# Moving a forget gate and its broadcast reads to an earlier place in a two-block hybrid attention kernel

## The chip, the cores and the metric

The kernel runs on one core of a Trainium2 chip. The metric is the device time of one execution in microseconds. Before the change the median of three runs is 1819.09 us, with 1818.62 and 1819.64 us as the lowest and highest.

## The reference

The program computes two blocks on a sequence of 512 tokens of 1024 features, in float32. The first block has two layers (`hybrid_layer`, l = 0 and 1). Each layer normalizes `x`, multiplies it by `w_in`, and feeds three kinds of attention: differential, stick-breaking and forgetting. Their outputs, gated by SiLU, are multiplied by `w_out`, normalized and added to `x`. The second block (a linear recurrence, a dilated attention and a feed-forward) is not touched here.

What matters here is the forgetting attention, and above all the cumulated log of its forget gate, which is added to the logits:

```python
log_f = jax.nn.log_sigmoid((ff + f_bias).astype(jnp.float32)).transpose(0, 2, 1)
cum_log_f = jnp.cumsum(log_f, axis=-1)
...
logits = jnp.einsum('bhqd,bhkd->bhqk', q[:, :, q0:q1], k[:, :, :q1]).astype(jnp.float32) * scale
logits = logits + cum_log_f[:, :, q0:q1, None] - cum_log_f[:, :, None, :q1]
```

`ff` holds 8 columns of the product with `w_in`, one for each of the 8 forgetting heads. The term of the query row falls out of the softmax, so the kernel adds only the key's term: one row of 512 numbers for each head.

## The kernel before, in words

**Products.** Every float32 operand is split into a high part (rounded, by ScalarE, line 219) and a low part (the rest, by VectorE and GpSimd, line 233), and each product is made of three TensorE products: high by high, high by low, low by high (`mm3`). Weights come in units of 128 x 1024 numbers: SP loads a unit into one of two `raw` buffers (line 203), and its parts go to one of four buffers of `wh` and `wl`. The normalized input stands in `hTH` and `hTL`, features on partitions.

**The order of the work.** The 12 head pairs of a layer (0 to 3 differential, 4 to 7 stick-breaking, 8 to 11 forgetting) each need three projections (`projections(n)`: q, k and the gate, one unit and 24 products of 512 columns each, called a chunk), and each two pairs need a value product (`values`, `value_steps`). The projections are generators that a filler (`Filler`) holds in one list in the order in which they were added: projections of pairs 1 to 11, with the value products of pairs 4, 6, 8 and 10 before the pair that needs them, and last the first half of the product with `w_out`. `spread` runs the attention steps of pair n, four of them, and between the stages of a step lets the filler go on up to a goal in chunks. The goals are such that the projections of pair 8 run while the attention steps of pair 7 do; the last of these projections is done shortly before the first attention step of pair 8.

Every TensorE product is made by `matmul` (line 126) or `transpose` (line 143), and both tie it behind the product written before, so TensorE's order is that of the Python program:

```python
def matmul(*args, **kw):
    tc.keep_in_program_order(nc.tensor.matmul(*args, **kw))
```

The other engines' instructions are ordered by a scheduler in the framework, which takes what is ready, the earlier written first; each engine then runs its list in order.

**The forget gate.** The value product of pair 8 has 264 columns instead of 256: the last 8 are the forget gates. `value_steps` adds the bias to them (line 569) into `ff`, 128 x 32. The generator `forget_gate` then makes softplus of it on VectorE with one Exp on ScalarE (`softplus_neg`, `log1p_exp_neg`, lines 480 to 503: one instruction each at lines 480, 484, 485, 487, 489, 491, seven pairs at lines 493 and 494, lines 495, 502 and 503), transposes the result by four TensorE transposes (line 639, recorded at line 143), copies and scans it on VectorE (lines 641 and 643) and writes it to the DRAM tile `cum` (line 645). In the kernel before, this generator is added after the three projections of pair 8.

**The broadcast reads.** In stage `a` of step 0 of each forgetting pair, `pair_step` has SP read one row of `cum` for each of the two heads, broadcast to 128 partitions (line 740), into tiles of the tag `bc`, which has four buffers; the forget gate uses two of these for its own input and output. Each score tile then gets the mask (line 747), and line 758 adds the broadcast and takes the row maximum. For a stick-breaking pair the score tile goes through lines 750 to 755. Stage `b_` transposes the weights and copies them (line 511), stage `c` makes the product with the values.

Of the kernel before, what the change touches and what calls it, by code (L numbers as in the profile page):

```python
# [16 lines left out]
P = 128  # L17
S = 512
# [70 lines left out]
def hybrid_kernel(ctx, tc, A, out):  # L89
    nc = tc.nc  # L90
# [11 lines left out]
    def nm(tag):  # L102
        count[0] += 1
        return f"{tag}_{count[0]}"
# [3 lines left out]
    def work(tag, dt=F32, shape=(P, S)):  # L108
        return ap.tile(list(shape), dt, tag=tag, bufs=BUFS[tag], name=nm(tag))
# [161 lines left out]
    def feature_steps(key, done, src=None, ps=None, span=(0, S)):  # L271

        wh, wl = key if isinstance(key[0], Slab) else unit(*key)
        if ps is None:
            ps = bank()
        nk = KD if src is None else len(src)
        lo, hi = span
        for k in range(nk):
            if src is None:
                mH, mL = hTH[:, k, lo:hi], hTL[:, k, lo:hi]  # L280
            else:
                mH, mL = src[k][0][:, lo:hi], src[k][1][:, lo:hi]
            c = slice(P * k, P * (k + 1))
            mm3(ps[:, lo:hi], wh[:, c], wl[:, c], mH, mL, k == 0, k == nk - 1)
            yield 1.27 * (hi - lo)
        if done is not None:
            done(ps)
# [284 lines left out]
    def hybrid_layer(l, vs0):  # L572
# [20 lines left out]
        st = {}  # L593

        def projections(n):

            kind, idx = n // 4, n % 4
            base = 4 * W_GRP * kind + P * idx
            s = st[n] = {}
            gens = []  # L600

            def put(name, scale):
                def done(ps):
                    pair = y_tile(F32R)
                    t = ps
                    if kind == 0:
                        t = work("e")
                        ACT.activation(t, ps, AF.Copy, scale=scale)
                        rope(t, P, shuffle8, cosT, sinT)
                    rest = None if name == "q" else klow[n % 2]  # L610
                    for b in range(2):
                        own = slice(64 * b, 64 * b + 64)
                        other = slice(64 - 64 * b, 128 - 64 * b)
                        cols = slice(S * b, S * b + S)
                        h = pair[own, cols]
                        lo = pair[other, cols] if name == "q" else rest[own, cols]
                        if kind == 0:
                            ACT.copy(h, t[own])
                            V.tensor_tensor(lo, t[own], h.bitcast(F32), op=ALU.subtract)  # L619
                        else:  # L620
                            ACT.activation(h, ps[own], AF.Copy, scale=scale)
                            V.scalar_tensor_tensor(lo, ps[own], scale, h.bitcast(F32), ALU.mult, ALU.subtract)
                        if name == "k":
                            evict(pair[other, cols], h.bitcast(F32))
                    s[name] = (pair, rest)

                return done

            def put_gate(ps):
                sg = work("sg")  # L630
                ACT.activation(sg, ps, AF.Tanh, scale=0.5)
                V.scalar_tensor_tensor(sg, sg, 1.0, ps, ALU.add, ALU.mult)
                s["sg"] = sg

            def forget_gate(ff):
                sp_f = softplus_neg(ff, 32)
                ffT = bank()
                for t in range(4):
                    transpose(ffT[0:8, P * t : P * (t + 1)], sp_f[:, 8 * t : 8 * t + 8])
                cum_in = work("bc")  # L640
                V.tensor_copy(cum_in[0:8], ffT[0:8])
                cum = work("bc")
                V.tensor_tensor_scan(cum[0:8], cum_in[0:8], cum_in[0:8], 0.0, ALU.add, ALU.bypass)
                st["cum"] = dp.tile([8, S], F32, tag="cum", bufs=2, name=nm("cum"))
                nc.sync.dma_start(st["cum"], cum[0:8])
                yield 0.0

            gens.append((CHUNK, feature_steps(("w_in", l, ((base, P),), 0, 8), put("q", 0.125))))
            gens.append((CHUNK, feature_steps(("w_in", l, ((base + W_GRP, P),), 0, 8), put("k", 1.0))))
            if kind == 0:  # L650
                s["vs"] = vs0[2 * (idx // 2) : 2 * (idx // 2) + 2]
            else:
                s["vs"] = st["vs", n - idx % 2]
            gens.append((CHUNK, feature_steps(("w_in", l, ((base + 3 * W_GRP, P),), 0, 8), put_gate)))
            if n == 8:
                gens.append((0.0, forget_gate(st["ff"])))
            return gens

        def values(n):
# [70 lines left out]
        def pair_step(n, i):  # L730
            s = st[n]
            loc = {}

            def a():
                if n >= 8 and i == 0:
                    s["bc"] = []
                    for b in range(2):
                        hd = 2 * (n - 8) + b
                        bc = work("bc")
                        nc.sync.dma_start(bc, st["cum"][hd : hd + 1, :].to_broadcast((P, S)))  # L740
                        s["bc"].append(bc)
                pss, w = scores(s, i)
                loc["w"] = []
                for b in range(2):
                    ps = pss[b]
                    mask = causal if n >= 8 else strict
                    V.tensor_tensor(ps[:, w - P : w], ps[:, w - P : w], mask, op=ALU.add)
                    e = work("e")
                    if n < 8:
                        ACT.activation(e[:, :w], ps[:, :w], AF.Sigmoid)  # L750
                        keep = work("e")
                        V.tensor_scalar(keep[:, :w], e[:, :w], -1.0, 1.0, ALU.mult, ALU.add)  # L752
                        rev = keep[:, :w][:, ::-1]
                        V.tensor_tensor_scan(rev, rev, rev, 1.0, ALU.mult, ALU.bypass)  # L754
                        V.tensor_tensor(e[:, : w - 1], e[:, : w - 1], keep[:, 1:w], op=ALU.mult)  # L755
                    else:
                        mx = stat()
                        V.tensor_tensor_reduce(e[:, :w], ps[:, :w], s["bc"][b][:, :w], 1.0, -3e38, ALU.add, ALU.max, mx)  # L758
                        V.tensor_scalar(mx, mx, -1.0, None, ALU.mult)  # L759
                        den = stat()  # L760
                        ACT.activation(e[:, :w], e[:, :w], AF.Exp, bias=mx, accum_out=den)  # L761
                        r = stat()
                        V.reciprocal(r, den)
                        V.tensor_scalar(e[:, :w], e[:, :w], r, None, ALU.mult)
                    loc["w"].append(e)

            def b_():
                if i == 0:
                    s["wT"] = {}
                for b in range(2):  # L770
                    if i == 1:
                        t = s["wT"][0, b]
                        transpose_evict(loc["w"][b], 2, dst=t[:, P : 3 * P])
                        s["wT"][1, b] = t[:, P : 3 * P]
                    else:
                        s["wT"][i, b] = transpose_evict(loc["w"][b], i + 1)

            def c():
                if i % 2 == 0:
                    return  # L780
                if i == 1:
                    s["o"] = bank()
                o = s["o"]
                for q in (i - 1, i):
                    for j in range(q + 1):
                        for b in range(2):
                            matmul(
                                o[64 * b : 64 * b + 64, P * q : P * (q + 1)],
                                s["vs"][n % 2][:, P * j + 64 * b : P * j + 64 * b + 64],
                                s["wT"][q, b][:, P * j : P * (j + 1)],  # L790
                                start=j == 0,
                                stop=j == q,
                            )
                if i == 3:
                    sg = s["sg"]
                    V.scalar_tensor_tensor(sg, o, 0.5, sg, ALU.mult, ALU.mult)
                    chunks[n] = split(sg, "yT")

            return [a, b_, c]
# [122 lines left out]
    vs0, gens = values0(0)  # L922
# [77 lines left out]
    for l in range(2):  # L1000
# [21 lines left out]
        if l == 0:  # L1022
            vs0, gens = values0(1)
# [7 lines left out]
    hd = {}  # L1031
# [448 lines left out]
```

## Time and profile before

| What | Value |
|---|---|
| median of 3 runs | 1819.09 us (1818.62 to 1819.64) |
| the profiled execution | 1817.58 us |
| its span | 1815.8 us |
| TensorE products (PE) | 1770.9 us busy |
| VectorE (DVE) | 1131.9 us busy |
| ScalarE (ACT) | 765.1 us busy |
| GpSimd (POOL) | 647.9 us busy |
| mean granted clock of TensorE | 0.992 |

Times in the profile are microseconds from the start of the span. L126 is line 126 of the kernel. In a row of the timeline the first number is the start, the second the time taken, then engine, line, operation, output and input tiles by their names (`ps` a PSUM bank, `sm` a small tile, `wT` a transposed weight tile), shapes and a count; a bracket at the end is the idle time of the engine just before, and what ended it. The granted clock is a share of TensorE's full 2.4 GHz. TensorE's busy time counts matmuls that overlap in the pipeline, so the distance between two starts says more than the duration of one.

### The profile page before, as it was taken

What the parts mean: (1) busy time and instruction counts of PE and PEld (TensorE: products, weight loads), DVE (VectorE), ACT (ScalarE), POOL (GpSimd) and SP (SyncE); (2) the same over time, 40 slices, a digit from 0 to 9 for tenths busy, and PEclk for the clock granted to TensorE, in tenths of its full rate; (3) what the DMA queues carried; (4) which work ended last, traced back from release to release, by engine and by line L of the source; (5) the groups of instructions that cost most, each with busy time, mean ns of one, the idle gap of its engine ahead of it and who ended that gap; (6) DMA issues with size and microseconds to landing.
All of it is one profiled execution on the core that took longest, in us unless ns stands there. A gap on an engine that the chain in (4) does not pass through costs nothing.

```text
span 1815.8 us, 26033 instructions
## 1 busy us (share of the span) xinstructions
PE 1770.9 (98%) x9774; PEld 1519.8 (84%) x9774; DVE 1131.9 (62%) x2450; ACT 765.1 (42%) x1461; POOL 647.9 (36%) x534
## 2 busy tenths in 40 slices
PE   9989998999998999899999999999999999999998
PEld 8778887888977888788899888878788888888898
DVE  5888898775588899776682677886433632222122
ACT  4545444443355544444433333677522432232221
POOL 3333212222333222122253555344554344444331
PEclk9999999999999999999999999999999999999999
DMA  5212222322321322222223223223323223332321
GB/s 202 92 47 82 65 76 82 93 70 72 123 76 53 93 60 70 94 93 83 71 88 116 82 77 99 82 71 105 110 83 117 97 93 93 103 95 94 103 94 70
DMA packets 51695, 162.12 MB, mean 89 GB/s; under 512 B 8481, under 2 KB 10049, under 8 KB 51570
## 3 DMA queue, kind: packets, MB, share of 16 engines
q1 hardware_dynamic: 51570, 160.46, 27.9%
q8 instruction: 77, 1.26, 0.3%
q14 instruction: 48, 0.39, 0.1%
HBM read 158.28 MB, written 2.16 MB: 88 GB/s over the span
## 4 chain that ended last, share of the span: by engine, by line
PE 76%; DVE 12%; ACT 3%; issue 3%; DMA 2%; POOL 2%; SPq 0%; POOLq 0%; DVEq 0%; ACTq 0%
PE ps L126 73%; PE ps L143 3%; DVE wl L233 2%; DVE e L754 1%; POOL e L522 1%; DMA raw<-in_wu_dram 1%; ACT wh L219 1%; DVE e L755 1%; DMA bc<-cum 1%; DVE e L520 1%; POOL st L361 1%; DVE yT L523 0%; DVE e L752 0%; DVE st L690 0%; DVE klow L619 0%
## 5 line engine op out<-in xcount | busy, mean ns | idle before, releaser
L233 POOL TENSOR_TENSOR wl<-raw,wh 128x368 fp32r<-128x368 f32 (+5 forms) x262 | 362.6, 1386 | 654.0 <-ACT wh L219 614.0
L126 PE MATMUL ps<-hTH,wh 128*128 128x512 f32 (+1 forms) x1336 | 533.2, 399 | 1.4 <-DVE sm L1128 1.4
L126 PE MATMUL ps<-hTH,wl 128*128 128x512 f32 (+1 forms) x1336 | 522.9, 391 | 0.0
L126 PE MATMUL ps<-hTL,wh 128*128 128x512 f32 (+1 forms) x1336 | 522.6, 391 | 0.0
L219 ACT CAST wh<-raw 128x1024 fp32r<-128x1024 f32 (+2 forms) x263 | 269.0, 1026 | 400.9 <-PE ps L126 227.7
L233 DVE TENSOR_TENSOR wl<-raw,wh 128x656 fp32r<-128x656 f32 (+6 forms) x261 | 257.9, 989 | 286.2 <-ACT wh L219 284.6
L126 PEld LDWEIGHTS ps<-hTH,wl 128*128 128x128 f32 x1336 | 253.0, 189 | 54.7
L126 PEld LDWEIGHTS ps<-hTH,wh 128*128 128x128 f32 x1336 | 253.9, 190 | 49.2 <-issue 1.6
L126 PEld LDWEIGHTS ps<-hTL,wh 128*128 128x128 f32 x1336 | 253.8, 190 | 47.1
L126 PE MATMUL ps<-wh,yT 128*128 128x512 f32 (+1 forms) x544 | 161.4, 369 | 0.0
L126 PEld LDWEIGHTS ps<-wh,yT 128*128 128x128 f32 x544 | 98.5, 189 | 15.9 <-issue 0.3
L126 PE MATMUL ps<-wh,hTH 128*128 128x256 f32 (+2 forms) x496 | 106.2, 302 | 3.1 <-DVE sm L716 1.6
L361 POOL TENSOR_TENSOR st<-st,half_neg 128x1 f32<-128x1 f32 x64 | 37.6, 587 | 196.0 <-DVE st L359 114.2
L126 PE MATMUL ps<-wl,hTH 128*128 128x256 f32 (+2 forms) x496 | 106.7, 300 | 0.4 <-POOL wl L233 0.4
L126 PE MATMUL ps<-wh,hTL 128*128 128x256 f32 (+2 forms) x496 | 105.3, 300 | 0.0
L126 PE MATMUL ps<-wl,yT 128*128 128x512 f32 (+1 forms) x272 | 99.2, 365 | 0.0
L126 PEld LDWEIGHTS ps<-wh,hTH 128*128 128x128 f32 x496 | 84.7, 208 | 4.9 <-DVE sm L716 2.0
L126 PEld LDWEIGHTS ps<-wl,hTH 128*128 128x128 f32 x496 | 84.5, 207 | 0.9 <-POOL wl L233 0.6
L126 PEld LDWEIGHTS ps<-wh,hTL 128*128 128x128 f32 x496 | 83.8, 207 | 0.1
L126 PE MATMUL ps<-y,y 128*128 128x128 f32 (+2 forms) x240 | 70.0, 323 | 12.4 <-DVE st L758 7.1
L143 PE MATMUL ps<-ident,e 128*128 128x128 f32 x460 | 71.8, 279 | 8.7 <-DVE st L357 6.0
L761 ACT ACTIVATE e<-e,st 128x128 f32<-128x128 f32 (+3 forms) x64 | 36.0, 562 | 85.7 <-DVE st L759 85.5
(331 smaller groups left out, 2877.5 us busy)
## 6 DMA issues: line engine op xcount, KB each, us to landing
raw<-in_wu_dram SPq DMA_DIRECT2D x263, 512.0 KB, 3.6
bc<-cum SPq DMA_DIRECT2D x16, 256.0 KB, 4.9
raw<-in_wu_dram SPq DMA_DIRECT2D x10, 256.0 KB, 2.6
yT<-back SPq DMA_DIRECT2D x8, 256.0 KB, 4.1
raw<-in_wu_dram SPq DMA_DIRECT2D x4, 396.0 KB, 3.2
x<-in_x_dram SPq DMA_DIRECT2D x3, 512.0 KB, 7.9
out_dram<-x SPq DMA_DIRECT2D x3, 512.0 KB, 2.6
gain<-in_post_norm_dram SPq DMA_DIRECT2D x2, 512.0 KB, 4.8
```

The lines of the kernel that those rows point to most:

```text
L126: tc.keep_in_program_order(nc.tensor.matmul(*args, **kw))
L143: tc.keep_in_program_order(nc.tensor.transpose(dst, src, ident))
L219: order(copy(h[:, : r.shape[1]], r))
L233: order(e.tensor_tensor(lo[:, d], r[:, d], h[:, d].bitcast(F32), op=ALU.subtract))
L361: order(G.tensor_tensor(r, m, half_neg, op=ALU.pow))
L520: V.stream_shuffle(sh[:n], t[:n], mask)
L522: G.tensor_tensor(shv, shv, sinT, op=ALU.mult)
L754: V.tensor_tensor_scan(rev, rev, rev, 1.0, ALU.mult, ALU.bypass)
L755: V.tensor_tensor(e[:, : w - 1], e[:, : w - 1], keep[:, 1:w], op=ALU.mult)
L761: ACT.activation(e[:, :w], e[:, :w], AF.Exp, bias=mx, accum_out=den)
```

## The change

The generator `forget_gate` is placed first among the generators of pair 8, ahead of the q projection. The two broadcast reads of each forgetting pair leave stage `a` of its first attention step and become a generator `forgets`, placed at index 2 of the pair's list: for pair 8 between its q and its k projection, for pairs 9, 10 and 11 between k and the gate.

```diff
+            def forgets(n, s):
+                s["bc"] = []
+                for b in range(2):
+                    hd = 2 * (n - 8) + b
+                    bc = work("bc")
+                    nc.sync.dma_start(bc, st["cum"][hd : hd + 1, :].to_broadcast((P, S)))
+                    s["bc"].append(bc)
+                yield 0.0
+
...
             gens.append((CHUNK, feature_steps(("w_in", l, ((base + 3 * W_GRP, P),), 0, 8), put_gate)))
             if n == 8:
-                gens.append((0.0, forget_gate(st["ff"])))
+                gens.insert(0, (0.0, forget_gate(st["ff"])))
+            if n >= 8:
+                gens.insert(2, (0.0, forgets(n, s)))
             return gens
...
             def a():
-                if n >= 8 and i == 0:
-                    s["bc"] = []
-                    for b in range(2):
-                        hd = 2 * (n - 8) + b
-                        bc = work("bc")
-                        nc.sync.dma_start(bc, st["cum"][hd : hd + 1, :].to_broadcast((P, S)))
-                        s["bc"].append(bc)
                 pss, w = scores(s, i)
```

## Rows read from the trace of the kernel before

**Rows 1.** The page's busy time of each engine, its share of the span, instructions.

```profile
PE 1770.9 (98%) x9774; PEld 1519.8 (84%) x9774; DVE 1131.9 (62%) x2450; ACT 765.1 (42%) x1461; POOL 647.9 (36%) x534
```

**Rows 2.** Waits, 255 to 330 and 700 to 770 us: total, times, longest.

```profile
DVE e L758 <- DMA bc<-cum: 4.2, 1, 4.2
...
DVE e L758 <- DMA bc<-cum: 3.6, 1, 3.6
```

**Rows 3.** Timeline of TensorE at the first attention steps of pair 8, both layers.

```profile
304.39 0.43 PE L126 MATMUL ps<-y,y 128*128 128x256 f32 x1 [4.36 <-DVE st L758]
...
304.84 0.63 PE L126 MATMUL ps<-hTH,wh 128*128 128x512 f32 x1
...
746.83 0.38 PE L126 MATMUL ps<-y,y 128*128 128x256 f32 x1 [2.78 <-DVE st L758]
```

**Rows 4.** Stretches of 4 us: PE, PEld, DVE, ACT, POOL busy, clock, DMA, GB/s.

```profile
304.00:308.00 4.00, 3.61 (x10) 2.93 (x11) 3.54 (x17) 1.95 (x6) 0.00 (x0) 0.57 0.55 216
...
730.00:734.00 4.00, 2.78 (x13) 2.39 (x14) 3.54 (x11) 2.19 (x4) 0.58 (x1) 0.66 0.08 32
734.00:738.00 4.00, 4.00 (x20) 3.34 (x19) 4.00 (x7) 0.74 (x3) 0.89 (x1) 0.92 0.00 0
...
746.00:750.00 4.00, 3.17 (x11) 2.26 (x11) 3.37 (x13) 0.87 (x4) 0.00 (x0) 0.79 0.65 257
750.00:754.00 4.00, 4.00 (x36) 3.49 (x36) 3.59 (x14) 3.78 (x10) 1.57 (x1) 0.78 0.11 14
```

**Rows 5.** Timeline of TensorE, two smaller stands between value product and pair 8.

```profile
287.85 1.35 PE L126 MATMUL ps<-wT,V 128*64 128x128 f32 x12 [0.65 <-DVE klow L622]
...
731.22 1.12 PE L126 MATMUL ps<-wT,V 128*64 128x128 f32 x6 [1.89 <-DVE wT L511]
```

**Rows 6.** Timeline of VectorE, layer 0, from the bias add through most of the chain.

```profile
265.72 0.14 DVE L569 TENSOR_TENSOR sm<-ps,sm 128x8 f32<-128x8 f32 x1
...
266.15 1.28 DVE L511 COPY wT<-ps 128x512 f32<-128x512 f32 x2
267.35 0.17 DVE L484 TENSOR_SCALAR sm<-sm 128x32 f32<-128x32 f32 x1
...
267.83 0.78 DVE L233 TENSOR_TENSOR wl<-raw,wh 128x656 fp32r<-128x656 f32 x1
268.52 0.96 DVE L487 TENSOR_TENSOR sm<-sm,sm 128x32 f32<-128x32 f32 x1
...
270.28 0.49 DVE L747 TENSOR_TENSOR ps<-ps,masks 128x128 f32<-128x128 f32 x2
...
272.00 0.19 DVE L493 TENSOR_TENSOR sm<-sm,sm 128x32 f32<-128x32 f32 x1
272.22 0.18 DVE L494 TENSOR_SCALAR sm<-sm 128x32 f32<-128x32 f32 x1
...
272.75 0.17 DVE L494 TENSOR_SCALAR sm<-sm 128x32 f32<-128x32 f32 x1
```

**Rows 7.** Timeline of TensorE: last value products of each layer, today's four transposes.

```profile
262.30 0.40 PE L126 MATMUL ps<-wl,hTH 128*128 128x264 f32 x2
...
284.52 0.60 PE L143 MATMUL ps<-ident,sm 128*8 128x128 f32 x4
...
703.84 0.40 PE L126 MATMUL ps<-wl,hTH 128*128 128x264 f32 x2
```

**Rows 8.** Timeline of ScalarE, layer 0: the chain's table load and its Exp.

```profile
265.13 1.28 ACT L482 ACT_TABLE_LOAD   x1
266.43 0.23 ACT L482 ACTIVATE sm<-sm 128x32 f32<-128x32 f32 x1
```

**Rows 9.** Timeline of VectorE, layer 1: the bias add and the chain's last instruction.

```profile
707.73 0.14 DVE L569 TENSOR_TENSOR sm<-ps,sm 128x8 f32<-128x8 f32 x1
...
721.12 0.19 DVE L503 TENSOR_TENSOR sm<-sm,sm 128x32 f32<-128x32 f32 x1
```

**Rows 10.** Timeline of SP: the broadcast reads as they are issued in layer 0.

```profile
298.48 1.85 SPq L740 DMA_DIRECT2D bc<-cum  x4
```

## The prediction, made before the changed kernel was run

> **What bounds the kernel now.** The busy table comes first: TensorE is busy for 98% of the span [rows 1], so time is won only where TensorE stands still or runs at its lower clock, and any new stand adds to the end in full. The waits come next. In each of the two layers VectorE waits once, 4.2 and 3.6 us, for a broadcast read of `cum` [rows 2]; these are the reads that the change moves. TensorE's timeline gives the price: its second score product of the first forgetting pair's step 1 waits 4.36 us in layer 0 and 2.78 us in layer 1 for VectorE's line 758 [rows 3], the instruction that waits for the broadcast. Right behind it, at 304.84 us, stand projection products (`hTH,wh`) that owe nothing to line 758; they too stood still. TensorE takes its products in the order written, and a late one holds all that follow.
>
> A stand has a tail. The table by stretches of 4 us shows the granted clock at 0.57 of 2.4 GHz from 304 to 308 us, right after layer 0's stand: part of that stretch ran at the lower level, 1.2 GHz, and (1-0.57) x 4 = 1.7 us of TensorE time went. After layer 1's stand it is 0.79 and 0.78 in two stretches, again (0.21+0.22) x 4 = 1.7 us [rows 4]. A smaller stand of 1.89 us at 731 us, where TensorE waited for VectorE's line 511 [rows 5], has 0.66 and 0.92 after it, (0.34+0.08) x 4 = 1.7 us [rows 4]. So 1.7 us is my price of a tail.
>
> **What the change removes.** With `cum` made three projection chunks earlier, the broadcasts have landed long before line 758 asks for them. VectorE's own wait [rows 2] is 0.16 us shorter than TensorE's in layer 0 and 0.8 us longer in layer 1, so without the read it would be ready about when TensorE comes to need it, and the whole stand and its tail go: 4.36 + 1.7 = 6.1 us in layer 0, 2.78 + 1.7 = 4.5 us in layer 1. Next late would be VectorE itself, by 0.16 us. Two more stands lie between the old and the new place, 0.65 us at 287.85 us and 1.89 us at 731.22 us, both for a VectorE that runs behind [rows 5]. The moved chain is some 5 us of VectorE work per layer (23 instructions that start 0.22 us apart when nothing comes between [rows 6]) that now competes in just these stretches. I take both stands as gone, with the second's tail: 0.65 + 1.89 + 1.7 = 4.2 us; kept is the other bound, 0. Removed in all: 6.1 + 4.5 + 4.2 = 14.8 us.
>
> **What it adds.** The forget gate is a generator that the filler runs in one go: 23 VectorE instructions and one Exp of ScalarE (lines 480 to 503), four TensorE transposes (line 639), a copy and a scan on VectorE (lines 641 and 643), one write of `cum`. Today the four transposes stand after the pair's third projection, at 284.52 us, and cost 0.60 us [rows 7]; the row shows no idle time, so their input was ready. After the change they stand right after the last value product, ahead of the pair's first projection. Line 143 ties every transpose, as line 126 every product, behind the last one written. The chain that feeds them begins with that value product, so TensorE must wait for the whole chain, and with it wait the first projection, the attention transposes behind that and all who read them; VectorE and ScalarE meanwhile work off what they are behind.
>
> How long? In layer 0 the last value products start at 262.30 and end at 262.70 us [rows 7]. VectorE, some work behind, adds the bias (line 569) at 265.72 us [rows 6], 3.0 us later. What comes ahead of it was written earlier, so I leave that unchanged. From there I walk the chain as it ran. Its sixth Horner step ends at 272.75 + 0.17 = 272.92 us; four instructions were still to come (lines 493, 494, 495, 503), 0.9 us at their cadence, so 273.8 us. That includes foreign work which the stand itself keeps away: the line 511 copies and the line 747 masks read TensorE output that is now behind the transposes. Line 484 could start when the Exp ends, at 266.66 [rows 8], instead of 267.35 us, 0.6 us sooner with a hand-over; the masks give 0.3 us back. The weight low halves (line 233, 0.78 us) and the one small instruction that took 0.96 us instead of 0.19 (line 487) [rows 6] I leave in. The chain is then done at about 272.9 us: a stand of 10.2 us. In layer 1 the value products end at 704.24 us [rows 7] and line 569 runs at 707.73 us [rows 9], 3.5 us later instead of 3.0, so 10.7 us. With a tail of 1.7 us each: 10.2 + 10.7 + 3.4 = 24.3 us.
>
> Bounds of this term. From below: nothing foreign at all, 0.8 + 0.8 us less, so 8.6 and 9.1 us; and if even the bias add ran straight after the value product, the chain alone, a table load of 1.28 us, an Exp of 0.23 us [rows 8] and 23 instructions at 0.22 us, is 6.6 us. From above: the chain at today's pace, with all the foreign work, ends in layer 1 at 721.31 us [rows 9], 17.1 us after the value product; I take layer 0 alike. I am nearest to the lower rows, because most of what slowed it cannot run while TensorE stands. Less than the chain alone is excluded, since every instruction reads the one before.
>
> ScalarE loads a table ahead of the Exp for 1.28 us, and the Exp starts 0.02 us after it [rows 8]. The Trainium skill, ScalarE: Activation LUTs, section What ACT_TABLE_LOAD costs, adds to such a load a drain of about the same length, some 2.66 us together. By that page the chain would be 1.4 us longer and the sum an estimated 2.8 us higher; this trace shows the load alone, and the sum goes by it.
>
> **The queues.** SP's in-order queue has the write of `cum` and then the broadcasts; today it issues four of these together at 298.48 us [rows 10], those of pairs 8 and 9, so for pair 9 nothing new is won, and pairs 10 and 11 wait for buffers of `bc` anyway. I cost the sixteen reads at nothing: the weight loads behind them are covered by the units already split, up to four, each worth 24 TensorE products; without that cover a wait like today's 4.2 us [rows 2] would show. GpSimd gets no work. The extra table switch is moved, not added; transposes, copy and scan cost what they cost.
>
> **Sum.** 24.3 - 14.8 = +9.5 us. The profiled execution took 1817.58 us (span 1815.8), so 1827.1 us; it stood 1.5 us below the median of 1819.09, so I give **1828.6 us** for the median.
>
> **Rivals.** *The chain keeps today's pace.* Weight low halves and attention work of pair 7 keep slipping in between its dependent instructions, as lines 233 and 487 did. Stands of 17.1 us: 2 x 18.8 - 14.8 = +22.8, 1842 us. Against it: much of that work needs TensorE's next outputs. Chance 0.09.
>
> *The chain is short.* The break-even stand is 14.8 / 2 - 1.7 = 5.7 us per layer; at the bound of 6.6 us the sum is 2 x 8.3 - 14.8 = +1.8, 1820.9 us, no measurable change (a measurement of this kernel tells about 0.2%, 3.6 us, from none). It needs VectorE not to be behind when the value product ends; the 3.0 and 3.5 us speak against it. Chance 0.08.
>
> *TensorE is not held: faster.* VectorE ran line 484 of the chain 17 us ahead of the transposes, so the order of issue need not be that of writing; were the first projection's products allowed past the waiting transposes, both new stands and tails would vanish and 14.8 us be won: 1804.3 us. It decides where the transposes' input comes less than 5.7 us after the value product or TensorE has other work for all but 5.7 us. Against it: lines 126 and 143, and the projection products that stood still behind one score product at 304.84 us [rows 3]. Chance 0.06.
>
> The forecast keeps 0.77; its own range is 1824 (stands of 8.6 and 9.1 us) to 1836 (stands 2 us longer, or the two VectorE stands of 4.2 us left). For 8 in 10 I take 1822 to 1836. Faster than the bound 0.06, within it 0.09, slower 0.85.
>
> **What would show it.** Right: a TensorE wait of 9 to 12 us on line 143 (`ident,sm`), released by line 503, right behind the last 264-wide value products in each layer, with a granted clock below 1 after it; line 758 no longer waiting for `bc<-cum`; the stands at 287.85 and 731.22 us gone; chain instructions packed at 0.22 us. Wrong: `ident,sm` transposes without idle time before them, or a wait for `bc<-cum` still there; a tail well away from 1.7 us would mis-size the sum but not turn it.

## The result, and the profile after

The changed kernel takes 1827.42 us (median of 6 runs, 1825.73 to 1828.84) where the kernel before, run beside it, takes 1817.84 us: a ratio of 1.0055, 95% interval 1.0045 to 1.0066. It is slower, by some 10 us (the interval is 8 to 12). The profiled execution took 1828.84 us with a span of 1827.1 us, 11.3 us over the profiled one of before.

The same 9774 products keep TensorE busy for the same time; the share of the span falls, as the page's busy line says (compare [rows 1]):

```profile
PE 1771.7 (97%) x9774; PEld 1521.5 (83%) x9774; DVE 1135.2 (62%) x2450; ACT 766.8 (42%) x1461; POOL 643.3 (35%) x534
```

So the 11 us are time in which TensorE stands (has no product to run) or runs slowly. Its timeline shows where. The first line is the end of layer 0's value product, the second the four transposes of the forget gate, the third the first projection product behind them, and the fourth the transposes in layer 1; the bracket is the idle time before the line:

```profile
262.59 0.40 PE L126 MATMUL ps<-wl,hTH 128*128 128x264 f32 x2
273.35 1.01 PE L143 MATMUL ps<-ident,sm 128*8 128x128 f32 x4 [10.35 <-DVE sm L503]
274.01 0.77 PE L126 MATMUL ps<-hTH,wh 128*128 128x512 f32 x1
...
721.24 1.01 PE L143 MATMUL ps<-ident,sm 128*8 128x128 f32 x4 [10.87 <-DVE sm L493]
```

There are two new stands, 10.35 and 10.87 us, and the transposes that did not wait before [rows 7] now wait for VectorE's line 503, the end of the softplus chain. Layer 1's bracket names line 493: that is an instruction of another chain, 8 columns wide, which slipped in beside; the gate's own chain ended at line 503 just ahead of it. The two stands between old and new place [rows 5] and the two for the broadcast reads [rows 3] are gone: no other product in these stretches of the two layers has idle time before it. The waits of line 762 (line 758 before) confirm the second: its list of what it sat idle for is empty, where there were two waits for `bc<-cum` [rows 2].

```profile
L762 DVE CUSTOM_DVE_ANT_0 e<-ps,bc x64: 265/475/692, 307.0 to 856.6; 128x128 f32<-128x128 f32 x16, 128x256 f32<-128x256 f32 x16, 128x384 f32<-128x384 f32 x16, 128x512 f32<-128x512 f32 x16
...
its engine sat idle before it (us, times) until:
who waited for it (us, times):
```

On VectorE's timeline the chain is seen from the bias add to its end, in layer 0. The bias add comes 3.0 us after the value product's end, as before [rows 6], and the chain runs packed, 7.2 us from the bias add to its end, with one weight low half (line 233) between and one instruction (line 502) stretched to 0.95 us:

```profile
265.98 0.14 DVE L569 TENSOR_TENSOR sm<-ps,sm 128x8 f32<-128x8 f32 x1
...
266.94 0.18 DVE L484 TENSOR_SCALAR sm<-sm 128x32 f32<-128x32 f32 x1 [0.46 <-ACT sm L482]
...
268.09 0.95 DVE L502 TENSOR_SCALAR sm<-sm 128x32 f32<-128x32 f32 x1
268.95 0.83 DVE L233 TENSOR_TENSOR wl<-raw,wh 128x656 fp32r<-128x656 f32 x1
269.71 0.18 DVE L493 TENSOR_TENSOR sm<-sm,sm 128x32 f32<-128x32 f32 x1
...
272.57 0.18 DVE L494 TENSOR_SCALAR sm<-sm 128x32 f32<-128x32 f32 x1
...
273.01 0.19 DVE L503 TENSOR_TENSOR sm<-sm,sm 128x32 f32<-128x32 f32 x1
```

The stretches of 4 us (columns as in [rows 4]; the clock is the third number from the right) show the tail. TensorE starts again at 273.35 and 721.24 us and finds the clock at 0.50, the lower of its two levels, where it stays for some 4 to 5 us:

```profile
270.00:274.00 4.00, 0.66 (x4) 0.43 (x5) 2.72 (x15) 0.00 (x0) 0.00 (x0) 0.50 0.42 133
274.00:278.00 4.00, 4.00 (x12) 3.02 (x11) 1.89 (x2) 0.00 (x0) 0.00 (x0) 0.50 0.02 4
278.00:282.00 4.00, 4.00 (x23) 3.48 (x22) 1.29 (x2) 0.00 (x0) 0.00 (x0) 0.96 0.61 208
...
718.00:722.00 4.00, 0.76 (x5) 0.53 (x5) 3.85 (x33) 0.12 (x1) 0.00 (x0) 0.50 0.44 131
722.00:726.00 4.00, 4.00 (x14) 3.13 (x13) 2.37 (x7) 0.00 (x0) 0.00 (x0) 0.57 0.02 4
```

Counted from the restart, that is 0.5 x 0.65 + 0.5 x 4 + 0.04 x 4 = 2.5 us in layer 0 and 0.5 x 0.76 + 0.43 x 4 = 2.1 us in layer 1.

The account between the two profiled executions: 10.35 + 10.87 us of new stands and 4.6 us of tails, 25.8 us; less the four stands and three tails that are gone, 14.8 us; that leaves 11.0 of the 11.3 us found. The tails that came are worth nearly as much as those that went (4.6 against 5.1 us); the loss is the longer stands.

### The profile page after: what moved, and what is told of

Same layout as the page of the kernel before. It is cut to its first block, busy times and chain, and to the rows that moved or that the text cites. A ratio compares the mean times of both kernels' runs of the same rounds, so it can differ in the third digit from the quotient of the medians.

```text
span 1827.1 us, 26039 instructions
## 1 busy us (share of the span) xinstructions
PE 1771.7 (97%) x9774; PEld 1521.5 (83%) x9774; DVE 1135.2 (62%) x2450; ACT 766.8 (42%) x1461; POOL 643.3 (35%) x534
## 4 chain that ended last, share of the span: by engine, by line
PE 83%; DVE 9%; issue 2%; ACT 2%; POOL 2%; DMA 1%; SPq 0%; POOLq 0%; DVEq 0%; ACTq 0%
PE ps L126 80%; PE ps L143 3%; DVE wl L233 1%; POOL e L522 1%; DVE st L701 1%; POOL st L361 1%; DVE e L520 1%; DVE e L758 0%; POOL wl L233 0%; DMA raw<-in_wu_dram 0%; DVE klow L619 0%; DMA x<-in_x_dram 0%; ACT wh L219 0%; DVE y L619 0%; DVE yT L523 0%
## 5 line engine op out<-in xcount | busy, mean ns | idle before, releaser
L233 POOL TENSOR_TENSOR wl<-raw,wh 128x368 fp32r<-128x368 f32 (+5 forms) x262 | 357.9, 1368 | 669.8 <-ACT wh L219 628.3
```

The costliest lines, as they stand in the source:

```text
L233: order(e.tensor_tensor(lo[:, d], r[:, d], h[:, d].bitcast(F32), op=ALU.subtract))
```

## Experiments

All are compared with the kernel before, run on the same chip beside them. A diff starts from the changed kernel where the text does not say that it starts from the kernel before.

**The reads alone.** The gate stays behind the three projections.

```diff
             if n == 8:
-                gens.insert(0, (0.0, forget_gate(st["ff"])))
-            if n >= 8:
+                gens.append((0.0, forget_gate(st["ff"])))
+                gens.append((0.0, forgets(n, s)))
+            if n > 8:
                 gens.insert(2, (0.0, forgets(n, s)))
```

> Only the reads move: the forget gate stays behind pair 8's three projections, pair 8's two reads follow it at once, the reads of pairs 9 to 11 go into their projections. Theory (the cost is TensorE's stand at the gate's early transposes): nothing is gained or lost, within 2 us of the kernel before; line 762 still waits some 4 us for a read of cum in each layer and TensorE stands 2.8 to 4.4 us there. Rival (the moved reads hold up SP's queue and cost the time): slower by several us, with waits for raw loads.

Measured: 1819.26 us against 1819.22, ratio 0.9999 (0.9988 to 1.0009). Layer 0's waits (total, times, longest; line 763 is the old 758):

```profile
PE ps L126 <- DVE st L763: 3.3, 1, 3.3
DVE e L763 <- DMA bc<-cum: 3.1, 1, 3.1
```

The wait for the read is still there, as it is in layer 1 with 2.6 us. SP's timeline shows what sets it:

```profile
296.48 0.30 SPq L645 DMA_DIRECT2D cum<-bc  x1
...
299.26 1.85 SPq L653 DMA_DIRECT2D bc<-cum  x4
```

The four reads go out 2.78 us after the write of `cum`, and in the kernel before it is 2.78 us too (295.70 to 298.48). Moving the reads alone is worth nothing; what they wait for is the gate. And more than its place made the gate late: in the kernel before the transposes run at 284.52 us, but VectorE, busy with attention work, makes the copy (line 641) and the scan (line 643) behind them only at 291.08 and 294.48 us, so the write comes 11 us after the transposes, against 3.0 us in the changed kernel:

```profile
291.08 0.65 DVE L641 COPY bc<-ps 8x512 f32<-8x512 f32 x1
...
294.48 1.19 DVE L643 TENSOR_TENSOR_SCAN bc<-bc 8x512 f32<-8x512 f32 x1
```

Giving only these two instructions an earlier turn was not tried.

**The gate alone.** The kernel before with the gate first among pair 8's projections, the reads left in the attention step.

```diff
             if n == 8:
-                gens.append((0.0, forget_gate(st["ff"])))
+                gens.insert(0, (0.0, forget_gate(st["ff"])))
```

> Only the forget gate moves to the front of pair 8's list; all reads stay in the first attention step. Theory: as slow as the changed kernel, 9 to 11 us over the kernel before, with the same stands of 10 to 11 us at the transposes and no wait for a read of cum. Rival (the reads cost the time): close to the kernel before or faster than it.

Measured: 1828.48 us, ratio 1.0048 (1.0034 to 1.0061), which holds the change's own 1.0055. The stands are those of the changed kernel:

```profile
273.75 1.01 PE L143 MATMUL ps<-ident,sm 128*8 128x128 f32 x4 [10.36 <-DVE sm L503]
...
721.04 1.01 PE L143 MATMUL ps<-ident,sm 128*8 128x128 f32 x4 [10.86 <-DVE sm L493]
```

No wait for a read of `cum` is left, though no read was moved. On SP the write and the reads go out as in the changed kernel, where they stand at 276.35 and 277.83 us, though these reads are still written in the attention step:

```profile
276.75 0.29 SPq L645 DMA_DIRECT2D cum<-bc  x1
278.22 1.76 SPq L740 DMA_DIRECT2D bc<-cum  x4
```

Within the interval the gate's place is the whole change, its loss and its gain.

**A longer chain.** If TensorE waits for the chain, a longer chain must lengthen the stand by its own length.

```diff
                 sp_f = softplus_neg(ff, 32)
+                for _ in range(28):
+                    V.tensor_scalar(sp_f, sp_f, 1.0, None, ALU.mult)
```

> The changed kernel with 28 more instructions in the chain, each multiplying the 128 x 32 softplus by 1.0 in place. Theory (TensorE waits for the whole chain): the stands grow by 28 x 0.2 to 0.22 = 5.6 to 6.2 us each, to 16 to 17 us, the total by 11 to 13 us over the changed kernel, some 21 to 23 us over the kernel before; the tail at the lower clock does not grow. Rival (TensorE's stand has another end, such as VectorE's backlog or a load): little change.

Measured: 1841.05 us, ratio 1.0121 (1.0102 to 1.0139), 21.8 us over the kernel before. TensorE's timeline, and the added instructions on VectorE's:

```profile
279.69 1.01 PE L143 MATMUL ps<-ident,sm 128*8 128x128 f32 x4 [16.46 <-DVE sm L638]
...
733.23 1.01 PE L143 MATMUL ps<-ident,sm 128*8 128x128 f32 x4 [16.96 <-DVE sm L638]
```

```profile
273.51 6.03 DVE L638 TENSOR_SCALAR sm<-sm 128x32 f32<-128x32 f32 x28
```

Both stands grew by 6.1 us for 6.03 us of chain. The tails, reckoned as above, are 2.9 and 1.4 us in place of 2.5 and 2.1: one is longer, one shorter, and their sum did not grow with the stands.

**A filled stand.** To price the tail alone, TensorE gets 40 products that nobody reads (they are recorded as 80 instructions in each layer), written ahead of the transposes; the chain and all else stay.

```diff
+                busy = bank()
+                for _ in range(40):
+                    matmul(busy[:, 0:P], ident, ident, start=True, stop=True)
                 for t in range(4):
                     transpose(ffT[0:8, P * t : P * (t + 1)], sp_f[:, 8 * t : 8 * t + 8])
```

> The changed kernel with 40 products of the identity by itself (128 x 128, into a PSUM bank that nothing reads) written between the last value product and the early transposes, so that TensorE has work in most of its stand of 10.4 and 10.9 us. Theory (a stand costs its length and a tail at the lower clock, 2.4 us in layer 0 and 2.1 us in layer 1 of the changed kernel): the transposes start no earlier, the granted clock stays at 1.0 behind them, and the total falls by 3 to 5 us against the changed kernel, to 1823 to 1825 us. Rival (the lower clock comes from something else in that stretch, or from the transposes): the tail stays and the total with it.

Measured: 1824.81 us, ratio 1.0032 (1.0020 to 1.0043), 4.1 us less over its kernel before than the changed kernel. The timeline and the stretch behind it:

```profile
261.15 9.09 PE L126 MATMUL ps<-ident 128*128 128x128 f32 x80
271.69 0.60 PE L143 MATMUL ps<-ident,sm 128*8 128x128 f32 x4 [1.45 <-DVE sm L503]
```

```profile
270.00:274.00 4.00, 2.55 (x16) 1.97 (x15) 2.95 (x9) 0.00 (x0) 0.00 (x0) 1.00 0.27 108
274.00:278.00 4.00, 4.00 (x24) 3.42 (x23) 1.54 (x3) 0.00 (x0) 0.00 (x0) 1.00 0.27 72
```

The transposes follow the chain as before, 10.4 us after the value product, but the clock stays at 1.00, in layer 1 too. The 4.1 us fit the 4.6 us of the two tails; the two intervals do not overlap, but they fix the difference only to some 3 us either way, so it is the clock that shows the tails gone. The rest of the loss is the stand.

**The gate after the k projection.** Late enough for the chain to run beside TensorE's work, early enough for the reads.

```diff
             if n == 8:
-                gens.insert(0, (0.0, forget_gate(st["ff"])))
-            if n >= 8:
+                gens.insert(2, (0.0, forget_gate(st["ff"])))
+                gens.append((0.0, forgets(n, s)))
+            if n > 8:
                 gens.insert(2, (0.0, forgets(n, s)))
```

> The forget gate goes between pair 8's k projection and its gate projection, two chunks later than in the changed kernel and one earlier than before; pair 8's reads come last in its list. Theory: the chain has some 16 us of TensorE work to run beside, so no stand over 0.5 us at the transposes, and the stands for the reads stay away: 8 to 12 us faster than the kernel before (1806 to 1810 us). Rival (the chain, given precedence on VectorE, costs the time wherever the transposes stand): slower than before.

Measured: 1808.74 us, ratio 0.9937 (0.9924 to 0.9951), about 10 us faster than the kernel before. The total came as expected, the stands did not: 2.08 and 2.07 us are left.

```profile
280.82 0.60 PE L143 MATMUL ps<-ident,sm 128*8 128x128 f32 x4 [2.08 <-DVE sm L503]
...
717.60 0.60 PE L143 MATMUL ps<-ident,sm 128*8 128x128 f32 x4 [2.07 <-DVE sm L493]
```

The chain now shares VectorE with pair 7's attention again and ends later for it. In layer 0 the value product and the chain end with

```profile
263.19 0.40 PE L126 MATMUL ps<-wl,hTH 128*128 128x264 f32 x2
```

```profile
280.48 0.19 DVE L503 TENSOR_TENSOR sm<-sm,sm 128x32 f32<-128x32 f32 x1
```

That is 17.1 us from the one to the other, as in the kernel before (17.1 us in both layers, [rows 7] and [rows 9] for layer 1). TensorE's work between covers 15.1 us of it, and the other 2 us are the stand.

With the reads left in the attention step and only the gate moved there, the one-line edit of the kernel before:

```diff
             if n == 8:
-                gens.append((0.0, forget_gate(st["ff"])))
+                gens.insert(2, (0.0, forget_gate(st["ff"])))
```

> The kernel before with one edit: the whole forget gate goes between pair 8's k and gate projection; all reads stay in the first attention step. Theory (where the reads are written is worth nothing): as fast as the version with the same place of the gate and moved reads, 1807 to 1810 us, with the same two stands of some 2 us. Rival (the reads had to be moved too): at least 2 us slower than that version, with a wait for a read of cum at line 758.

Measured: 1809.2 us, ratio 0.9947 (0.9934 to 0.9960), with stands of 2.06 us in both layers and no wait for a read. Once more no effect of the reads' place is seen.

**The chain first, its transposes later.** Does VectorE's backlog or the chain's rank make the 2 us stands? Rank means that the scheduler prefers on VectorE what is written earlier.

```diff
                 sp_f = softplus_neg(ff, 32)
+                st["sp_f"] = sp_f
+                yield 0.0
+
+            def forget_rest():
+                sp_f = st["sp_f"]
                 ffT = bank()
...
             if n == 8:
                 gens.insert(0, (0.0, forget_gate(st["ff"])))
-            if n >= 8:
+                gens.insert(3, (0.0, forget_rest()))
+                gens.append((0.0, forgets(n, s)))
+            if n > 8:
                 gens.insert(2, (0.0, forgets(n, s)))
```

> The gate in two parts: the chain (bias to softplus, lines 480 to 503) stays at the front of pair 8's list as in the changed kernel, the transposes, copy, scan and write go between the k and the gate projection; pair 8's reads come last in its list. Theory: the chain, written early, has precedence on VectorE and is done some 11 us after the value product, as in the changed kernel, before TensorE reaches the transposes; the 2.08 us stands of the version with the whole gate there vanish, and it is 3 to 5 us faster than that version, 1803 to 1806 us. Rival (it is the chain's precedence on VectorE that costs): not faster than that version, with TensorE waiting for VectorE's attention work instead.

Measured: 1810.09 us, ratio 0.9952 (0.9939 to 0.9964), no gain on the version above. The theory missed half of it:

```profile
277.87 0.60 PE L143 MATMUL ps<-ident,sm 128*8 128x128 f32 x4
289.65 0.98 PE L126 MATMUL ps<-wT,V 128*64 128x128 f32 x8 [1.87 <-DVE wT L511]
...
726.69 0.65 PE L126 MATMUL ps<-wT,V 128*64 128x128 f32 x6 [2.56 <-DVE wT L511]
```

The chain ends 12.5 and 13.5 us after the value product and the transposes no longer wait, but TensorE waits 1.87 and 2.56 us for VectorE at line 511 some 12 us later. The rival had this right: here the early rank only changed which of VectorE's work came late. It also shows that the early rank is not what costs the changed kernel its 10 us, since this version has the same rank and is 0.5% faster than the kernel before.

**The chain on GpSimd.** Then a lighter VectorE should help. The gate stands after k, and 21 of the 23 VectorE instructions of the gate's softplus go to GpSimd.

```diff
-    def log1p_exp_neg(x, w):
+    def log1p_exp_neg(x, w, E=V):
...
-            V.tensor_tensor(p, p, z2, op=ALU.mult)
-            V.tensor_scalar(p, p, 2.0 / n, None, ALU.add)
+            E.tensor_tensor(p, p, z2, op=ALU.mult)
+            E.tensor_scalar(p, p, 2.0 / n, None, ALU.add)
...
-                sp_f = softplus_neg(ff, 32)
+                sp_f = softplus_neg(ff, 32, G)
```

> The version with the whole gate between pair 8's k and gate projection, and 21 of the chain's 23 VectorE instructions given to GpSimd (all but lines 480 and 485). Theory (VectorE's backlog is what is left in these stretches, the 2 us stands at the transposes and whatever takes their place): VectorE is some 4.6 us less loaded per layer, the stands fall below 0.5 us and the total by 2 to 5 us against that version, to 1804 to 1807 us. Rival (GpSimd is slower per instruction and its weight halves queue behind the chain): 21 instructions of 0.3 to 0.6 us, 6 to 13 us, end later than VectorE's chain did, the stands stay at 2 us or grow, and the total does not fall.

Measured: 1806.95 us, ratio 0.9934 (0.9920 to 0.9947). TensorE's timeline:

```profile
279.36 0.60 PE L143 MATMUL ps<-ident,sm 128*8 128x128 f32 x4
...
714.10 0.60 PE L143 MATMUL ps<-ident,sm 128*8 128x128 f32 x4 [0.20 <-POOL sm L503]
726.26 0.65 PE L126 MATMUL ps<-wT,V 128*64 128x128 f32 x6 [2.10 <-DVE wT L511]
```

Layer 0 has no stand left, nor another in its place. In layer 1 the transposes wait 0.20 us, but the line 511 stand is there with 2.10 us; there the second block's own softplus (8 columns, called in line 966) still runs on VectorE, until some 7 us before the stand begins. That this is what keeps the stand was not tried. Against the version with the whole gate after k the gain is within the two intervals, so the 2 to 5 us expected are not shown.

## Why the prediction was right

It forecast 9.5 us more, from the mechanism that the runs bear out; 10 us were found. That the number is so near is partly luck: its terms as measured give 11.0 us, stands of 21.2 instead of 20.9 us and tails of 4.6 instead of 3.4, and the two profiled executions differ by 11.3.

**The stand.** The step said that the transposes hold TensorE for the whole chain and gave 10.2 and 10.7 us; the profile shows 10.35 and 10.87, and the longer chain moved both by its own length. The start of the chain, taken over from before, was right: the bias add came 3.0 us after the value product again, 3.4 in layer 1. The two interruptions that I left in, one low half and one stretched instruction, were both there, at other places of the chain. The size lay much nearer to this walk than to either bound. But one step of it is not argued: the last four instructions are put at their cadence, to 273.8 us, where in the kernel before the chain ended 6 us later:

```profile
279.57 0.19 DVE L503 TENSOR_TENSOR sm<-sm,sm 128x32 f32<-128x32 f32 x1
```

Attention work, the low half of a weight and others came between there. In the changed kernel none of it did, as the forecast has it, but its price stood only in the upper bound.

**The removed stands** went as forecast, all four, together 9.68 us. Why layer 1's 1.89 us went is not shown. The forecast put it down to the chain competing with VectorE's work in that stretch, but the version with the chain first has its chain done 3.6 us sooner than the kernel before, counted from the value product, and stands 2.56 us there; what fits all the runs is that VectorE catches up where TensorE stood, or ran products that nobody reads, for 2 us or more shortly before. That the reads of pairs 8 to 11 win nothing by their own move is borne out by the first two experiments. SP's queue showed no price either: in both layers' stretches no engine waits for a weight load.

**The tail** was the term that was off: 1.7 us each in the forecast, 2.5 and 2.1 us in the profile. It was read from three stands that happened to agree. In the filled stand the clock stays up and the total falls by some 4 us, so the step is sound, but its size is not a constant.

**The rivals.** TensorE is held: no projection product passed the waiting transposes. The chain neither kept the old pace, which would have made stands of 17.1 us, nor came down to 6.6 us. The Exp again follows its table load at once:

```profile
265.39 1.28 ACT L482 ACT_TABLE_LOAD   x1
266.68 0.23 ACT L482 ACTIVATE sm<-sm 128x32 f32<-128x32 f32 x1
```

The drain that the Trainium skill (ScalarE: Activation LUTs, What ACT_TABLE_LOAD costs) adds to a table load does not show here either; with the 1.4 us more that the prediction drew from that page it would have missed both stands.

**The range.** Its ends do not follow from their grounds: stands of 8.6 and 9.1 us give 1825.4 us for the median and not 1824, and either ground of the upper end gives 1833 and not 1836. The measured time lies within the narrower ends too.

What the prediction did not see is how near a better place was. It asked only what the two given places cost. The chain needs 17.1 us where TensorE's work runs beside it, which is its own upper bound, and two projections cover all but 2 us of that.

## What to carry to other kernels

On an engine that runs in the order written, moving a step earlier moves its wait along: ask when its input is ready, from the last producer through every dependent instruction, and put the step no earlier than that. Here 23 small VectorE instructions, most of them 0.2 us and invisible in the busy table, made a chain that ended 10.4 us after its input while TensorE stood, and 17.1 us after it while TensorE worked. Of the three places tried the best was two projections after the input and one before the old place. When a transfer is late, look first at what feeds it: moving the reads alone changed nothing that could be measured, moving what they read made the whole difference.

## What the runs showed that was not expected

The tail at the lower clock is no fixed price. Stands of 2.78 and 1.89 us in layer 1 had 1.7 us of tail each in the kernel before [rows 4]. With only the reads moved, layer 1 stood 1.91 and 2.79 us at the same two places, with no tail at all:

```profile
732.00:736.00 4.00, 2.20 (x16) 1.88 (x17) 3.52 (x12) 1.61 (x3) 0.00 (x1) 1.00 0.18 73
736.00:740.00 4.00, 4.00 (x21) 3.35 (x20) 4.00 (x6) 2.33 (x5) 1.48 (x1) 1.00 0.00 0
746.00:750.00 4.00, 1.66 (x8) 1.45 (x9) 1.96 (x6) 1.82 (x4) 0.00 (x0) 1.00 0.98 295
750.00:754.00 4.00, 4.00 (x40) 3.18 (x40) 3.57 (x18) 2.80 (x7) 1.30 (x1) 1.00 0.40 156
```

In the same run layer 0's stand of 3.31 us has a tail of 3.1 us, counted from the restart:

```profile
304.00:308.00 4.00, 3.88 (x10) 3.21 (x11) 3.57 (x18) 2.23 (x6) 0.17 (x1) 0.50 0.71 249
308.00:312.00 4.00, 4.00 (x35) 3.09 (x35) 3.53 (x11) 2.17 (x8) 1.39 (x1) 0.71 0.39 101
```

The traces of these runs and of the kernel before have twelve stands of 1.9 to 2.8 us in these stretches of the two layers: four had a tail of 1.6 to 1.7 us, eight had none. One of the four is in layer 0 of the one-line version with the gate after k; the same stand of 2.1 us in the version with moved reads has none. The six stands above 10 us without the filling products all had one, of 1.4 to 2.9 us. For a stand of 2 or 3 us a tail is a possibility, to be put into the range rather than into the sum. Also, GpSimd did the 128 x 32 instructions of the chain in mostly 0.25 to 0.30 us, single ones in up to 0.96, against VectorE's 0.18 to 0.19, less of a difference than I had reckoned with.
